# A two-layer hybrid decoder on one core: first phase, one gate block and the last products in another order, the last 256 rows written through transposes

## The chip, the cores and the metric

The kernel runs on one core of a Trainium2 chip. The metric is the device time of one execution in microseconds (us); lower is better. Engines are named as in the profile: PE is the matrix engine (TensorE), PEld its weight loads, DVE is VectorE, ACT is ScalarE, POOL is GpSimd and SP is SyncE, which here only issues DMAs. "L390" is line 390 of the kernel before.

## What is computed

The trunk has 1024 tokens, width 1024 and two layers; all in fp32. Cut to what matters here:

```
h = x
for layer in (0, 1):
    hn = rms_norm(h, mix_norm[layer])
    h  = h + (rg_lru_block(hn) if layer == 0 else stick_breaking_attention(hn))
    h  = h + swiglu_ffn(rms_norm(h, ffn_norm[layer]))
return rms_norm(h, final_norm)

rg_lru_block(x):                       # layer 0
    u = x @ w_in + b_in;  gate, rec = u[:1024], u[1024:]
    rec = causal depthwise conv of 4 taps over rec
    r, i = sigmoid(block-diagonal gates of rec, 4 blocks of 256)
    log_a = -8 * r * softplus(-lam);  a = exp(log_a);  b = sqrt(1 - a*a) * i * rec
    s[t] = a[t] * s[t-1] + b[t]
    return (gelu(gate) * s) @ w_out + b_out

swiglu_ffn(x): (silu(x @ w_gate) * (x @ w_up)) @ w_down          # 2816 wide
```

## The kernel before

**Data.** Activations are held transposed: a tile is 128 channels by 512 tokens. There are 8 channel tiles (d or k from 0 to 7) and two token halves n, so the residual stream is `h[d][n]`. Each fp32 operand is split into a high part (a copy on ACT, `whi`, `xh`, `rh`) and a low part (a subtraction on DVE, `wlo`, `xl`, `rl`), and each product is three matmuls (`mm3`, L124 to L127: high by high, high by low, low by high). An RMS norm is a sum of squares over channels: ACT squares, DVE adds the squares into an accumulator, PE sums over partitions (`column_stats`, L189), a chain of one ACT square root and six small DVE operations makes the factor per token (`rstd`, L158 to L167, into `rcol`), and PE spreads the factor over all partitions by multiplying it with the identity (`spread`, L172).

**First phase** (L245 to L320). All engines follow an order written out by hand. SP loads the eight x tiles of half 0 (`xr`) alternating with eight weight pieces (`fr`, the first four column tiles of `w_in`); ACT's queue loads the table of vectors `vc` (gains, biases). For each k, ACT and DVE split weights and x and PE multiplies half 0. Then PE does half 1 of the four tiles (`second(i, ks)`, 24 matmuls each), between which the two column sums and the two spreads are placed: sum 0, spread 0 after half a tile, sum 1 after one and a half tiles, spread 1 after two and a quarter. The norm is linear, so the tiles are multiplied by the factor (`rbc[n]`) afterwards.

**The RG-LRU stage** (L323 to L475). PE's order is a list of words written by hand (L472); the order of the other engines follows from a planner in the order of the program. A word is a letter and a number: `A` projects a recurrent tile (48 matmuls, unless the first phase did it), multiplies it by `rbc` (L400), runs the four taps (L402, L404) and splits the result (`rh` L406, `rl` L407). `G` is a gate block: it multiplies two recurrent tiles, 2b and 2b+1, with the gate weights (48 matmuls) and then needs a long chain of ACT and DVE operations for each, ending in a scan (L428 to L439). `B` projects a gate-branch tile, multiplies by `rbc` (L446) and applies gelu. `Y` multiplies scan and gelu (DVE). The order ends in

```
... A6 B3 Y3 G2 A7 B4 Y4 G3 B5 Y5 B6 Y6
```

after which `last_tile` (L454) projects B7 and rewrites `xh`, `xl` with the split products, tile by tile; the output projection (`ob_ps`) reads them. Weight tiles come from a ring of three pairs; PSUM has four tiles of 1024 columns, used in turn. The tiles of this stage, small ones included, lie in a pool `lp` over the memory of the first phase, and a tile waits until what lay there is no longer read. The small tiles hold the softplus constants (36 short DVE operations, L331 to L365).

**FFN and end.** The FFNs use a seven-product scheme of 2x2 blocks: a step of the second matrix (a "visit", `VISITS`) updates channel tiles d and d+4 in both halves with products 0 to 6. Products 0, 2, 4 and 5 use one PSUM bank in turn, so each waits until ACT or DVE has read the one before (`post_out`, L995). A channel tile that is complete is squared, added into `acc[n]` and multiplied by the final gain (`finished`, L984). In the last layer the last two visits, to tiles 3 and 7 and to tiles 0 and 4, are written out by hand: products 0, 1, 2, 4, 5 of visit 11 in a loop, the rest in `finish` (L1175 to L1230). There the last visit is done with plain products (`last`), first for half 0 (`first`), then for half 1 in two pieces of 256 tokens (`mid`, `end`); for each piece the factor is computed and spread, and `give` multiplies all eight channel tiles (DVE, or POOL for the tiles called slow) and stores them by SP. For `end` this is four matmuls (L1229), eight multiplications of 128x256 and eight stores, alternating between SP and ACT. The output is stored transposed as (8, 2, 128, 512).

Of the kernel before, what the change touches and what calls it, by code (L numbers as in the profile page):

```python
# [29 lines left out]
V_MIX, V_FFN, V_FIN, V_BIN, V_CW, V_CB, V_GB, V_LAM, V_BO = 0, 16, 32, 40, 56, 88, 96, 112, 120  # L30
FIRST = (ND, ND + 1, 0, ND + 2)
# [3 lines left out]
def trunk(  # L35
# [14 lines left out]
    nc = tc.nc  # L50
    f32 = lambda t: t.bitcast(F32)
# [192 lines left out]

    with ExitStack() as st, tc.manual_schedule(engines={E.PE, E.Activation, E.DVE, E.Pool, E.SP}):  # L245
# [7 lines left out]
        xr = [[one(f"xr{d}_{n}") for n in range(NH)] for d in range(ND)]  # L253
        nc.scalar.dma_start(vc, table)
        for k in range(ND):
            nc.sync.dma_start(xr[k][0], x[k, 0])
            nc.sync.dma_start(fr[k].rearrange("p (t c) -> p t c", t=4), lru_first[k])
# [17 lines left out]

        bank = half(pa[FIRST[3]], 1)
        for k in range(ND):
# [14 lines left out]
        for k in range(3):  # L292
            x_square(k, 1)

# [22 lines left out]
        second(2, range(2))  # L317
        spread_to(1)
        second(2, range(2, ND))
# [3 lines left out]
    with ExitStack() as st:  # L323
        lp = st.enter_context(tc.tile_pool(name="lp", bufs=1, reuse_waits="tile"))
        V = nc.vector
        lam = vc[:, V_LAM : V_LAM + ND]
        sm = lambda name: lp.tile([P, ND], F32, name=name)
# [12 lines left out]
        two = lp.tile([P, ND], I32, name="two")  # L340
# [15 lines left out]
        nbias = lp.tile([P, ND, 4], F32, name="nbias")  # L356
# [114 lines left out]
        with tc.manual_schedule(engines={E.PE}):  # L471
            for what in "A0 A1 B0 A2 B1 G0 A3 Y0 Y1 A4 B2 G1 A5 Y2 A6 B3 Y3 G2 A7 B4 Y4 G3 B5 Y5 B6 Y6".split():  # L472
                {"A": stage_a, "B": stage_b, "G": stage_g, "Y": stage_y}[what[0]](int(what[1]))
            mix = last_tile(ND - 1)
# [65 lines left out]
    def mix_out_ffn_in(h, mix, bias, layer, gnext, ob):  # L540
# [128 lines left out]
        with tc.manual_schedule(engines={E.PE, E.Activation, E.DVE, E.Pool}):  # L669
# [325 lines left out]
            def post_out(u, i, ps):  # L995
# [11 lines left out]
                if VISITS[u][2] == NF // 2 and i in ((1, 3, 6, 5) if final and u == NV - 2 else (1, 4, 6, 5)):  # L1007
# [3 lines left out]
            if final:  # L1011
                steps.pop()
# [3 lines left out]

            last_use = {p: max(u for u, (_, p0, p1) in enumerate(VISITS) if p0 <= p < p1) for p in range(NF // 2)}
            for s_, (kind, x) in enumerate(steps):
                w, nw, ahead = nw, nxt, None
                if s_ + 2 < len(steps):  # L1020
                    ahead = weights_of(*steps[s_ + 2])
                elif final and s_ + 2 == len(steps):
                    ahead = weights_out(NV - 1)
                    ahead.homes = held[1:]
                last_two = final and kind == "v" and x == NV - 2
# [15 lines left out]
                def tail(i, js):  # L1041
                    if i == 3:
                        banks[2] = pp.tile([P, NB], F32, tag="p", name=f"p{i}_ps")
                    part(banks[2], w, i, rhs[i], js, onto=i != 3)
                    if js[-1] == 2:
                        post_out(x, i, banks[2])
                        for dn in done:
                            finished(*dn)
                        del done[:]

                if last_two:
                    early = cp.tile([P, 4], F32, tag="rs_s", name="rs_s", bufs=2)
                    nc.scalar.sqrt(early[:, 0:1], ones)
                rest = [lambda: tail(3, range(3)), lambda js: tail(6, js)]
                for k, i in enumerate((0, 1, 2, 4, 5) if last_two else ORDER):
# [42 lines left out]
                    elif nw and last_two:  # L1098
                        if k == 3:
                            nw.a_lo()  # L1100
                            nw.r_hi()
                        elif k == 4:
                            nw.r_lo()
# [63 lines left out]
            if final:  # L1167
                finish(h, nw, R, pp, ob, held[0], *rest)
# [5 lines left out]

    def finish(h, w, R, pp, ob, rs, third, sixth):  # L1175
        d0, p0, p1 = 0, NF // 2 - 2, NF // 2


        def last(x, n, i0, i1, between=lambda: None, while_squared=lambda: None):
            d, cs = d0 + x * HK, slice(i0 * P, i1 * P)  # L1180
            ps = pp.tile([P, NB], F32, tag="p", name="o_ps")[:, cs]
            for k, p in enumerate(range(p0, p1)):
                for y in range(2):
                    hi, lo = w.a[("r", y) if x else y]
                    c = slice(k * P, (k + 1) * P)
                    rhs = [t[:, cs] for t in R[p][((0, 1), (7, 6))[n][y]]]
                    mm3(ps, hi[:, c], lo[:, c], *rhs, k + y == 0, k + y == 2)
            between()
            t, sq, ac = h[d][n][:, cs], rbc[n][:, cs], acc[n][:, cs]
# [392 lines left out]
```

## Time and profile before

| | us |
|---|---|
| median of three runs | 2222.49 (2217.23 to 2222.87) |
| profiled execution, device time | 2223.05 |
| its span, first to last instruction | 2221.3 |
| PE busy | 2172.0 (98%) |
| DVE busy | 1722.2 (78%) |
| ACT busy | 1147.8 (52%) |
| POOL busy | 224.2 (10%) |

The span is the distance from the first to the last instruction of one execution; 1.75 us of its device time lie outside. Times in the profile are counted from the start of the span. Busy time of PE counts each matmul to its modelled end, so that PE can be called busy while it runs at half clock.

### The profile page before, as it was taken

The numbers are of one execution on the slowest core, as the hardware profiler recorded it, in microseconds if no ns is written. First come the engines' busy times: TensorE is split into PE (matmuls) and PEld (weight loads), VectorE is DVE, ScalarE is ACT, GpSimd is POOL, SyncE is SP. The second block draws the span as 40 slices with busy tenths as digits, with TensorE's granted clock in tenths as the row PEclk, the third lists the DMA queues.
The fourth block names the chain that finished last, engine by engine and source line by source line (L and its number), as shares of the span: only waits on it lengthen the run. The fifth ranks groups of instructions, "written<-read, shape, count | busy, mean of one in ns | idle before, by whom it ended". The sixth has DMA issues, their size and how long they took to land.

```text
span 2221.3 us, 28188 instructions
## 1 busy us (share of the span) xinstructions
PE 2172.0 (98%) x10022; PEld 1798.9 (81%) x10022; DVE 1722.2 (78%) x2418; ACT 1147.8 (52%) x2030; POOL 224.2 (10%) x356
## 2 busy tenths in 40 slices
PE   8998999999999999999999999999999999999996
PEld 7787888888888888878888888778888888888885
DVE  6877678677777887868888888866876777788886
ACT  5567444444444554646666666653543444454464
POOL 0000020000000000003333333421000000000001
PEclk9999999999999999999999999999999999999998
DMA  4020312344444854443333333631133444466442
GB/s 172 21 63 31 133 40 70 108 126 146 142 156 133 284 185 120 151 133 86 89 93 99 101 87 104 196 118 57 48 113 118 149 142 147 152 234 226 135 136 81
DMA packets 132893, 273.51 MB, mean 123 GB/s; under 512 B 15376, under 2 KB 23696, under 8 KB 132752
## 3 DMA queue, kind: packets, MB, share of 16 engines
q1 hardware_dynamic: 132032, 271.12, 38.8%
q8 instruction: 79, 1.29, 0.2%
q10 hardware_dynamic: 720, 0.59, 0.1%
q14 instruction: 62, 0.51, 0.1%
HBM read 175.70 MB, written 70.78 MB: 111 GB/s over the span
## 4 chain that ended last, share of the span: by engine, by line
PE 80%; DVE 11%; ACT 5%; issue 2%; DMA 1%; SPq 0%; DVEq 0%; ACTq 0%
PE p_ps L127 18%; PE p_ps L125 18%; PE p_ps L126 17%; PE qk_ps L127 3%; PE qk_ps L125 3%; PE qk_ps L126 3%; PE ob_ps L125 2%; PE ob_ps L126 2%; PE ob_ps L127 2%; PE wt_ps L1404 2%; DVE F L1392 2%; PE a_ps L125 1%; PE a_ps L126 1%; PE a_ps L127 1%; PE z_ps L1367 1%
## 5 line engine op out<-in xcount | busy, mean ns | idle before, releaser
L1393 POOL TENSOR_TENSOR w<-w,F 128x128 f32<-128x128 f32 (+1 forms) x192 | 185.1, 965 | 316.7 <-DVE F L1390 179.5
L125 PE MATMUL p_ps<-vh,wbh 128*128 128x512 f32 x524 | 204.4, 390 | 1.4 <-ACT ta L1002 0.8
L125 PE MATMUL p_ps<-vh,wch 128*128 128x512 f32 x524 | 204.2, 390 | 0.8 <-ACT tb L1002 0.8
L127 PE MATMUL p_ps<-vh,wcl 128*128 128x512 f32 x524 | 204.1, 390 | 0.5 <-DVE wcl L629 0.5
L127 PE MATMUL p_ps<-vh,wbl 128*128 128x512 f32 x524 | 204.2, 390 | 0.0
L127 PE MATMUL p_ps<-vh,wal 128*128 128x512 f32 x524 | 204.1, 389 | 0.1
L126 PE MATMUL p_ps<-vl,wbh 128*128 128x512 f32 x524 | 203.9, 389 | 0.0
L126 PE MATMUL p_ps<-vl,wch 128*128 128x512 f32 x524 | 203.9, 389 | 0.0
L126 PE MATMUL p_ps<-vl,wah 128*128 128x512 f32 x524 | 203.9, 389 | 0.0
L125 PE MATMUL p_ps<-vh,wah 128*128 128x512 f32 x524 | 203.8, 389 | 0.0
L615 ACT CAST wbh<-sb 128x1024 fp32r<-128x1024 f32 (+2 forms) x69 | 69.6, 1009 | 192.6 <-DVE sb L599 192.6
L1413 ACT CAST th<-wt_ps 128x512 fp32r<-128x512 f32 x192 | 93.3, 486 | 72.2 <-PE wt_ps L1404 70.0
L1390 DVE TENSOR_TENSOR_SCAN F<-F,unit 128x128 f32<-128x128 f32 (+3 forms) x128 | 127.1, 994 | 4.5 <-ACT F L1386 4.5
L1414 DVE TENSOR_TENSOR tl<-wt_ps,th 128x512 fp32r<-128x512 f32 x192 | 105.1, 548 | 28.6 <-ACT th L1413 27.3
L125 PE MATMUL qk_ps<-vh,whi 128*128 128x512 f32 x264 | 118.9, 451 | 0.6 <-ACT vh L205 0.6
L125 PEld LDWEIGHTS p_ps<-vh,wbh 128*128 128x128 f32 x524 | 98.4, 188 | 22.4 <-ACT ta L1002 1.2
L127 PEld LDWEIGHTS p_ps<-vh,wcl 128*128 128x128 f32 x524 | 98.4, 188 | 21.8 <-DVE wcl L629 1.4
L127 PEld LDWEIGHTS p_ps<-vh,wbl 128*128 128x128 f32 x524 | 98.4, 188 | 21.8 <-DVE wbl L619 1.3
L125 PEld LDWEIGHTS p_ps<-vh,wch 128*128 128x128 f32 x524 | 98.4, 188 | 21.5 <-ACT tb L1002 1.3
L127 PEld LDWEIGHTS p_ps<-vh,wal 128*128 128x128 f32 x524 | 98.4, 188 | 21.4 <-DVE wal L610 1.0
L126 PEld LDWEIGHTS p_ps<-vl,wah 128*128 128x128 f32 x524 | 98.4, 188 | 20.4
L126 PEld LDWEIGHTS p_ps<-vl,wch 128*128 128x128 f32 x524 | 98.4, 188 | 20.4
(402 smaller groups left out, 5706.3 us busy)
## 6 DMA issues: line engine op xcount, KB each, us to landing
raw<-in_ffn_w_in SPq DMA_DIRECT2D x88, 512.0 KB, 3.8
vl<-pd SPq DMA_DIRECT2D x128, 256.0 KB, 3.7
pd<-U SPq DMA_DIRECT2D x90, 256.0 KB, 2.3
raw<-in_ffn_w_out SPq DMA_DIRECT2D x28, 512.0 KB, 4.0
raw<-in_attn_w_qkv SPq DMA_DIRECT2D x24, 512.0 KB, 3.6
acc<-pd SPq DMA_DIRECT2D x28, 256.0 KB, 2.7
pph<-rbc SPq DMA_DIRECT2D x28, 256.0 KB, 2.5
ppl<-acc SPq DMA_DIRECT2D x28, 256.0 KB, 2.6
```

The source lines that it names most:

```text
L125: nc.tensor.matmul(ps, lhsT=wh, rhs=mh, start=first, stop=False, **kw)
L126: nc.tensor.matmul(ps, lhsT=wh, rhs=ml, start=False, stop=False, **kw)
L127: nc.tensor.matmul(ps, lhsT=wl, rhs=mh, start=False, stop=last, **kw)
L615: nc.scalar.copy(self.full(self.wb), self.full(self.sb))
L1367: nc.tensor.matmul(ps[:, 0 : c1 - c0], lhsT=lhsT, rhs=KL[q][hx][:, c0:c1], start=False, stop=True)
L1390: nc.vector.tensor_tensor_scan(rev, rev, unit[:, NB - n :][:, ::-1], first, op0=ALU.mult, op1=ALU.add)
L1392: nc.vector.tensor_tensor_scan(rev, rev, rev, first, op0=ALU.mult, op1=ALU.bypass)
L1393: nc.gpsimd.tensor_mul(wt, wt, F[:, 1 : n + 1])
L1404: nc.tensor.transpose(tp[:, c : c + P], W[q, hx, j, kb // 4][:, (kb % 4) * P : (kb % 4 + 1) * P], ident)
L1413: nc.scalar.copy(th[:, q0:], tp[:, q0:])
L1414: nc.vector.tensor_sub(tl[:, q0:], tp[:, q0:], f32(th)[:, q0:])
```

## The change

1. **First phase.** The first weight piece `fr[0]` is issued on ACT's queue, ahead of the table, and no longer on SP's. PE gets eight products of the identity with itself ahead of the first real product. All squares and sums of half 1 come before the first `column_stats`. Sum 1 now comes after the first tile of half 1 and spread 1 half a tile later.
2. **Small tiles.** The small tiles of the RG-LRU stage get a pool of their own, `lc`, opened ahead of the first phase.
3. **Gate blocks.** `B5` moves ahead of `G3`, so that three tiles (A7, B4, B5) lie between G2 and G3.
4. **End.** Visits 11 and 12 are both in a new `finish`. Its products alternate: 0, 1, 2 of visit 11, tile 0 of visit 12 (half 0), 4, tile 4 (half 0), 5, 3, tile 0 (mid), 6, and so on. The squares go to a tile of their own. The last 256 tokens are not multiplied tile by tile: 16 transposes turn them into two row tiles of 128 tokens by 1024 channels in four PSUM banks, ACT and DVE multiply each bank by the token's factor on the way out (`rcol`, one number per partition), and four stores write rows.
5. **Output.** The output is one flat array: 768 tokens transposed, then 256 tokens as rows.

```diff
+        nc.scalar.dma_start(f4(fr[0]), lru_first[0])
         nc.scalar.dma_start(vc, table)
         for k in range(ND):
             nc.sync.dma_start(xr[k][0], x[k, 0])
-            nc.sync.dma_start(fr[k].rearrange("p (t c) -> p t c", t=4), lru_first[k])
+            if k:
+                nc.sync.dma_start(f4(fr[k]), lru_first[k])
...
         bank = half(pa[FIRST[3]], 1)
+        for i in range(8):
+            nc.tensor.matmul(bank[:, 0:P], lhsT=ident, rhs=ident, start=True, stop=True)
...
-        for k in range(3):
+        for k in range(ND):
             x_square(k, 1)
+            x_add(k, 1)
...
         column_stats(sacc[0], bank, 0)
-        for k in range(3, ND):
-            x_square(k, 1)
-        for k in range(ND - 2):
-            x_add(k, 1)
         second(0, range(4))
         spread_to(0)
-        for k in (ND - 2, ND - 1):
-            x_add(k, 1)
         second(0, range(4, ND))
+        column_stats(sacc[1], bank, 1)
         second(1, range(4))
-        column_stats(sacc[1], bank, 1)
+        spread_to(1)
         second(1, range(4, ND))
-        second(2, range(2))
-        spread_to(1)
-        second(2, range(2, ND))
+        second(2, range(ND))
         second(3, range(ND))
...
-        sm = lambda name: lp.tile([P, ND], F32, name=name)
+        sm = lambda name: lc.tile([P, ND], F32, name=name)
...
-... G2 A7 B4 Y4 G3 B5 Y5 B6 Y6
+... G2 A7 B4 Y4 B5 G3 Y5 B6 Y6
...
+                post = product(2)
+                post()
+                finished(d1, 0)
+                w.d_hi()
+                w.d_lo()
+                e.r_hi()
+                e.r_lo()
+                sq = rp.tile([P, D], F32, tag="raw", name="sq")
+                last(0, *first)
+                post = product(4)
+                summed(0, *first)
+                post()
+                last(1, *first)
+                post = product(5)
+                summed(1, *first)
+                post()
+                post = product(3)
+                finished(d1 + HK, 0)
+                post()
+                last(0, *mid)
+                stats(acc[0], pp, "p", 0)
+                finished(d1 + HK, 1)
+                summed(0, *mid)
+                post = product(6)
+                factor(*first)
+                give(*first, (), (3, 7))
+                post()
+                give(*first, (1, 2))
+                last(1, *mid)
+                finished(d1, 1)
+                give(*first, (5,))
+                summed(1, *mid)
+                last(0, *end)
+                give(*first, (0,), (4,))
+                summed(0, *end)
+                stats(acc[1], pp, "p", 1, 0, 2)
+                give(*first, (6,))
+                last(1, *end)
+                factor(*mid)
+                give(*mid, (), (3, 7))
+                summed(1, *end)
+                rows = [(hf, i, pp.tile([P, NB], F32, tag="p", name="e_ps")) for i in range(2, 4) for hf in range(2)]
...
+                turn((1, 2, 3))
+                give(*mid, (1, 2))
+                stats(acc[1], pp, "p", 1, 2, 4)
+                turn((0,))
+                ys = [rp.tile([P, D], F32, tag="raw", name="y") for _ in range(2)]
+                for k, (hf, i, ps) in enumerate(rows):
+                    y = half(ys[i - 2], hf)
+                    r = rcol[:, NT // 2 + i : NT // 2 + i + 1]
+                    if k % 2 == 0:
+                        nc.scalar.activation(y, ps, AF.Copy, scale=r)
+                    else:
+                        V.tensor_scalar_mul(y, ps, r)
+                    (nc.scalar if k % 2 else nc.sync).dma_start(
+                        out_r[(i - 2) * P : (i - 1) * P, hf * NB : (hf + 1) * NB], y
+                    )
+                    if k == 1:
+                        give(*mid, (5, 6), (0, 4))
```

In the new `finish`, `w` holds the weights of visit 11 and `e` those of visit 12; `last(x, n, i0, i1)` does tile 4x of visit 12, adds it into `h` and squares it, and `summed` adds the square and applies the gain. `turn(js)` transposes the 128x128 pieces of channel tiles j and j+4.

More of the change, by code (lines that the diff above doesn't have):

```diff
@@ L339, in trunk @@
             V.scalar_tensor_tensor(pq, pq, cf, gq, op0=ALU.add, op1=ALU.mult)
-        two = lp.tile([P, ND], I32, name="two")
+        two = lc.tile([P, ND], I32, name="two")
         V.tensor_scalar(two, kq, -8388608.0, 127.0 * 8388608.0, op0=ALU.mult, op1=ALU.add)
@@ L471, in trunk @@
         with tc.manual_schedule(engines={E.PE}):
-            for what in "A0 A1 B0 A2 B1 G0 A3 Y0 Y1 A4 B2 G1 A5 Y2 A6 B3 Y3 G2 A7 B4 Y4 G3 B5 Y5 B6 Y6".split():
+            for what in "A0 A1 B0 A2 B1 G0 A3 Y0 Y1 A4 B2 G1 A5 Y2 A6 B3 Y3 G2 A7 B4 Y4 B5 G3 Y5 B6 Y6".split():
                 {"A": stage_a, "B": stage_b, "G": stage_g, "Y": stage_y}[what[0]](int(what[1]))
@@ L1021, in mix_out_ffn_in @@
                     ahead = weights_of(*steps[s_ + 2])
[L1022 to L1025, printed above, removed]
+                    if final and s_ + 3 == len(steps):
+                        ahead.homes = held[1:]
                 g = {5: (0, 1), 6: (2, 3)} if s_ == 0 else {0: (1,), 1: (2,), 2: (3,)}
@@ L1040, in mix_out_ffn_in @@
                     rhs = {i: [R[p][i] for p in range(p0, p1)] for i in range(NPROD)}
[L1041 to L1055, printed above, removed]
+                for k, i in enumerate(ORDER):
                     b = BANK[i]
```

142 lines of the change are left out of this document (74 added, 68 removed).

## The prediction

> **What bounds the kernel now.** I read the page, then who waited for whom on PE, stage by stage, then the timeline around each wait. The page's line of busy times:
>
> ```profile
> PE 2172.0 (98%) x10022; PEld 1798.9 (81%) x10022; DVE 1722.2 (78%) x2418; ACT 1147.8 (52%) x2030; POOL 224.2 (10%) x356
> ```
>
> PE is the bound, and it is idle for only 2% of the span. The change takes no product out of the long middle, so what it can win is PE's waits in the stages that it touches, the slow clock behind them, and the stretch behind PE's last instruction. PE's waits from 0 to 100 us, from 100 to 250, and from 2150 to the end (total us, times, longest):
>
> ```profile
> PE a_ps L125 <- ACT xh L262: 5.9, 1, 5.9
> PE g_ps L125 <- ACT rh L406: 1.2, 1, 1.2
> PE g_ps L126 <- DVE rl L407: 0.8, 1, 0.8
> ...
> PE g_ps L125 <- ACT rh L406: 6.2, 1, 6.2
> PE g_ps L126 <- DVE rl L407: 0.5, 1, 0.5
> ...
> PE st_ps L191 <- DVE acc L1193: 3.5, 2, 1.9
> PE ob L172 <- DVE rcol L167: 2.2, 1, 2.2
> PE ob L172 <- DVE hh L1208: 2.1, 1, 2.1
> PE p_ps L125 <- ACT tb L1002: 1.5, 2, 0.8
> PE p_ps L125 <- ACT ta L1002: 1.4, 2, 0.8
> ```
>
> These are all of PE's waits there. G0 waits (1.2 + 0.8) and G3 (6.2 + 0.5). G1 and G2, each with three tiles between it and the gate block ahead, do not appear. The end waits 10.7. Two windows (length, then busy time of PE, PEld, DVE, ACT, POOL; granted clock; DMA) show G3's stretch and what lies behind PE's last row:
>
> ```profile
> 180.00:200.00 20.00, 13.37 (x52) 10.32 (x51) 19.70 (x17) 10.63 (x10) 0.00 (x0) 0.81 0.14 38
> ...
> 2214.30:2221.30 7.00, 0.00 (x1) 0.00 (x0) 2.08 (x6) 0.37 (x1) 1.41 (x2) 0.50 0.48 158
> ```
>
> At G3 the clock falls to 0.81 while DVE is full (19.70 of 20); at the end 7.0 pass without PE.
>
> **G3 and B5, the largest term.** PE's timeline (start, duration, instruction, idle before):
>
> ```profile
> 188.98 0.39 PE L127 MATMUL a_ps<-xh,wlo 128*128 128x512 f32 x1
> 189.20 0.39 PE L125 MATMUL g_ps<-rh,whi 128*128 128x512 f32 x1
> ...
> 196.21 0.79 PE L125 MATMUL g_ps<-rh,whi 128*128 128x512 f32 x1 [6.16 <-ACT rh L406]
> ...
> 198.06 0.63 PE L127 MATMUL g_ps<-rh,wlo 128*128 128x512 f32 x1
> ...
> 210.02 0.39 PE L125 MATMUL a_ps<-xh,whi 128*128 128x512 f32 x1
> ```
>
> At full speed products start about 0.227 apart (188.98 to 189.20, to a hundredth), so the block's 48 should take 10.9; it took 210.02 - 189.20 = 20.8. So 9.9 are lost: 6.6 of waits, and by subtraction 3.3 because the rows behind the wait run at half clock (0.63 long against 0.39). A7's parts, a weight split and the two ends of G3's chain:
>
> ```profile
> 195.11 1.04 ACT L406 CAST rh<-rec 128x1024 fp32r<-128x1024 f32 x1 [4.88 <-DVE rec L404]
> 196.19 1.22 DVE L407 TENSOR_TENSOR rl<-rec,rh 128x1024 fp32r<-128x1024 f32 x1
> ...
> 190.04 1.20 DVE L116 TENSOR_TENSOR wlo<-raw,whi 128x1024 fp32r<-128x1024 f32 x1
> ...
> 205.95 1.23 DVE L431 TENSOR_TENSOR gs<-gs,rec 128x1024 f32<-128x1024 f32 x1 [6.08 <-ACT gs L429]
> 226.97 2.29 DVE L439 TENSOR_TENSOR_SCAN y<-ga,gs 128x1024 f32<-128x1024 f32 x1
> ```
>
> With B5 in between, PE works from 189.2 to 200.1. A7's parts are complete at 196.15 and 197.41, so G3 no longer waits. B5's weights were split at 190.04; now they come ahead of G3's in the ring and get the slot of G2's weights, free since PE left G2, while G3's gate weights get the later place, done by 191.2 and wanted at 200.1. The whole 9.9 goes.
>
> Late next: the output projection. In the old times G3 ends at 211.0, 1.0 later than before, but only B6 and the last tile (2 x 10.9) follow, so the projection begins at 232.8 instead of 210.0 + 3 x 10.9 = 242.7. It wants the last split part of half 0 seven k steps (0.68 each) later, at 237.6. Rows for what lies on the way:
>
> ```profile
> 201.32 1.28 ACT L428 ACT_TABLE_LOAD   x1 [2.71 <-PE g_ps L127]
> 202.62 1.11 ACT L428 ACTIVATE ga<-g_ps,vc 128x1024 f32<-128x1024 f32 x1
> ...
> 227.36 1.16 ACT L447 ACTIVATE gb<-gb,vc 128x1024 f32<-128x1024 f32 x1
> ...
> 231.98 1.29 DVE L446 TENSOR_TENSOR gb<-a_ps,rbc 128x512 f32<-128x512 f32 x2 [1.60 <-PE a_ps L127]
> 236.19 1.89 DVE L466 TENSOR_TENSOR xl<-y,xh 128x512 fp32r<-128x512 f32 x3
> ```
>
> From 200.1 on ACT waits for B5's eviction (1.3), loads a table, does the gelu, loads again and does three activations of 1.1: G3's chain starts at 208.4 instead of 205.95. It took until 229.26, 23.3; B5's eviction and one weight split (2.5) no longer lie inside it, so it ends at about 229.2 again. By 237.6 DVE then still owes B6's eviction and Y6 (2.5), B7's eviction and product of half 0 (1.3), a weight split (1.2) and eight parts (0.6 each): 9.8, to 239.0, or 1.4 late. I take 1.5 back; bounds 0 (DVE slips small pieces into pauses of the chain) and 4 (the second weight tile also falls behind). **Term: -9.9 + 1.5 = -8.4** (-5.9 to -9.9).
>
> The Trainium skill, "ScalarE: Activation LUTs", section What ACT_TABLE_LOAD costs, counts a load of 1.28 and a drain of about 1.38, 2.66 for each switch. By that two switches would start the chain 2.8 later and the term would be about -5.6. The trace does not show the drain: the activation above starts 1.30 after its load.
>
> **G0 and the first phase.** G0's waits are 1.9. Why A1 is late:
>
> ```profile
> 46.77 0.69 DVE L302 COPY rbc<-a_ps 128x512 f32<-128x512 f32 x1 [3.73 <-PE a_ps L172]
> 51.34 0.17 DVE L331 SCALAR_TENSOR_TENSOR az<-vc 128x8 f32<-128x8 f32 x1 [3.88 <-PE a_ps L126]
> ```
>
> Spread 1 stands 18 products further forward, so its copy comes 4.1 earlier, at 42.7. Then DVE waited 3.88 for PE, because the small tiles lie over weight pieces that PE still reads; with `lc` that goes. A0 and A1 start about 8 earlier, where 2 are wanted. What the move costs: seven sums of half 1 (0.6 each, 4.2) stand ahead of sum 0's chain on DVE, and PE waits for that chain at spread 0, half a tile (2.7) later. The weight splits that DVE can put off (wanted from G0 and B1 on) cover it; without that cover it is 1.5. **Term: -1.9** (-0.4 to -2).
>
> The start:
>
> ```profile
> 1.18 0.42 SPq L257 DMA_DIRECT2D fr<-in_lru_first  x1
> ...
> 4.59 0.62 ACT L278 CAST fh<-fr 128x512 fp32r<-128x512 f32 x1 [2.13 <-DMA fr<-in_lru_first]
> ...
> 5.88 0.80 PE L125 MATMUL a_ps<-xh,fh 128*128 128x512 f32 x1 [5.88 <-ACT xh L262]
> ...
> 11.52 0.43 PE L125 MATMUL a_ps<-xh,fh 128*128 128x512 f32 x1
> ```
>
> The piece was issued second on SP; now it goes first on ACT's queue, one issue (0.42) sooner, but the table, which x's high part needs, goes one later. Gain 0 to 0.4; I take 0.4. The eight identity products last 2.4 at half clock (the row of 2213.08 below has four in 1.22), then PE idles about 2 until the data come. Full speed came 5.6 after the first product here and 6.6 after 196.21, so 2.4 of work and a pause should hardly hasten it. Bounds: nothing, or full clock from the first product on, half of 5.6. I take 0.3, near the first. **Term: -0.7** (0 to -3.2).
>
> **The end.** PE's first row behind the shared products, its last two groups, the last factor and the last multiplications; below, transposes in the attention stage:
>
> ```profile
> 2176.30 0.50 PE L125 MATMUL p_ps<-vh,wbh 128*128 128x512 f32 x1 [0.75 <-ACT ta L1002]
> ...
> 2209.93 1.01 PE L191 MATMUL st_ps<-ones,acc 128*128 128x1 f32 x4 [1.55 <-DVE acc L1193]
> 2213.08 1.22 PE L172 MATMUL ob<-ident,rcol 128*128 128x128 f32 x4 [2.14 <-DVE hh L1208]
> ...
> 2212.20 0.16 DVE L167 TENSOR_TENSOR rcol<-rs_s,rs_t 128x2 f32<-128x2 f32 x1
> 2214.74 2.08 DVE L1208 TENSOR_TENSOR hh<-hh,ob 128x256 f32<-128x256 f32 x6 [1.72 <-ACT held L1199]
> ...
> 1201.28 0.60 PE L1404 MATMUL wt_ps<-ident,w 128*128 128x128 f32 x4
> ```
>
> From 2176.30 to 2214.30 PE spends 38.0, of which 10.7 - 0.8 = 9.9 waiting and 28.1 working. Removed: the last spread, 1.2. Added: 16 transposes, at 0.11 each about 1.8 (four end within 0.60). The alternation puts other products between those that share a bank and between a tile and its sum, so PE restarts less often: I take 1 for that. Work 27.7. Stepping through the new order with durations like those above leaves waits of about 3.5: 0.8 where the first tile of visit 12 waits for its low weights behind four DVE operations, 2 at the sum of `mid`, 0.7 at its spread. Product 2 starts 0.9 later, because the square and gain left from the visit before now go ahead of the table load on ACT. PE ends at 2177.2 + 27.7 + 3.5 = 2208.4; the last sum starts 1.1 earlier, at 2207.3, and from sum to factor it is 2212.36 - 2209.93 = 2.4, so 2209.7. Two evictions on DVE (0.69, as in the row of L302) with two multiplications of 0.4 between take 2.1, ACT's two (half of 1.11 each) less: 2211.8. Before, from the last multiplication (2216.8) to the end of the span it was 4.5, with eight stores behind the factor; now four follow, but SP's stand behind stores of tiles that POOL multiplies. I take 4: 2215.8. **Term: -5.5** (-3 if the waits stay at 6; -8.5 if there are none).
>
> **Sum.** -8.4 - 1.9 - 0.7 - 5.5 = -16.5. The profiled execution took 2223.05, 0.6 above the median, so 2206.5 by it and **2206** against the median of 2222.49.
>
> **Rivals.** (a) DVE becomes the bound: G3's wait returns as one of about 5.5 at the output projection. For: no slack is left in the arithmetic above. Against: bits of DVE work can fill pauses. 2206 + 4 = 2210. (b) The identity products bring the clock up early and DVE keeps up: 2.5 and 1.5 more, and 2 at the end: 2200. (c) The clock falls at the end: PE pauses there and 16 transposes at half clock take 1.8 more: 2208. The four rows of 2213.08 took 1.22 against 0.60 for four transposes among other products; no row shows transposes alone. The Trainium skill, "TensorE: Matmul & The Clock Gate", Part 4, says that a transpose does not count as activity for the clock, which speaks for (c). (d) Slower: at the output projection DVE comes later than PE at each of its first four products, by 2 each, and each pause brings half clock as behind 196.21, 3.3 more: 4 x 5.3 = 21, so 2227. It decides from four pauses on; against it, DVE makes a part in 0.6 and PE uses one in 0.68, so DVE should catch up. (e) The move does nothing, because A7's parts slip as far as G3 does: 2206 + 8.4 = 2214.
>
> **Chances.** Forecast 0.56, (a) 0.18, (b) 0.12, (c) 0.06, (d) 0.04, (e) 0.04. Below 0.3% (6.7 us, about what a measurement here can tell from no change) counts as the same, so faster ends at 2215.8. The forecast, (a), (b), (c) and (e) lie there; 0.05 is left for the edges of (a) and (e) beyond it. Faster 0.91, same 0.05, slower 0.04. All terms at their ends give -9.3 and -23.6, 2213 and 2199; I go one lower for (b), whose clock gain could fall together with an end without waits: 2198 to 2213. That leaves out (d), (e) and some edges.
>
> **What would show it.** Right: no PE wait over 1 at G3, and matmul rows of 0.39 from G0 to the output projection; the operations on `lc` tiles before 46 us; PE waits below 5 in the last 40 us; no spread for the last 256 tokens; a first real product near 5.5 and rows of 0.63 for 5 us behind it. Wrong: a wait at `ob_ps` over 3 (a), several of them (d), rows of 0.39 before 9 us (b), transposes 0.2 apart (c), G3 still waiting for `rh` (e), a wait at spread 0 (the G0 term).

## The result: no difference that can be measured

The changed kernel took 2217.72 us (median of 19 runs, 2214.07 to 2220.24), the kernel before on the same chip 2218.75 (19 runs, 2214.69 to 2222.87): ratio 0.9993, 95% interval 0.9985 to 1.0. Forecast were 2206 and a range from 2198 to 2213. G0's and G3's waits are gone as forecast, and nearly all of the gain is lost again, most of it at a place that no part of the prediction names. The profiled execution took 2218.56 (span 2216.8). The page's line of busy times:

```profile
PE 2177.2 (98%) x10050; PEld 1805.3 (81%) x10050; DVE 1721.9 (78%) x2412; ACT 1152.7 (52%) x2033; POOL 224.1 (10%) x356
```

PE is no less busy than before (2172.0). Its waits in the same three stretches as before (total us, times, longest):

```profile
PE a_ps L129 <- DVE xl L272: 1.6, 1, 1.6
PE a_ps L285 <- POOL ident masks.py:199: 1.4, 1, 1.4
PE a_ps L175 <- DVE rcol L170: 1.2, 1, 1.2
PE a_ps L128 <- ACT xh L269: 1.1, 1, 1.1
...
PE a_ps L130 <- DVE wlo L119: 5.6, 1, 5.6
PE ob_ps L129 <- DVE xl L467: 0.2, 1, 0.2
...
PE st_ps L194 <- DVE acc L1047: 3.1, 1, 3.1
PE p_ps L128 <- ACT ta L1003: 2.0, 1, 2.0
```

No row for `rh` or `rl` is left: the moves did what they say. New are a wait of 1.6 at the second real product, one of 1.2 at spread 0, and one of 5.6 for the low part of a weight tile. PE's timeline at the start, around that last wait, and at the end:

```profile
1.36 3.78 PE L285 MATMUL a_ps<-ident 128*128 128x128 f32 x16 [1.36 <-POOL ident masks.py:199]
6.20 0.80 PE L128 MATMUL a_ps<-xh,fh 128*128 128x512 f32 x1 [1.06 <-ACT xh L269]
8.57 0.80 PE L129 MATMUL a_ps<-xl,fh 128*128 128x512 f32 x1 [1.58 <-DVE xl L272]
...
103.90 0.39 PE L129 MATMUL a_ps<-xl,whi 128*128 128x512 f32 x1
109.84 0.79 PE L130 MATMUL a_ps<-xh,wlo 128*128 128x512 f32 x1 [5.56 <-DVE wlo L119]
110.44 0.63 PE L128 MATMUL a_ps<-xh,whi 128*128 128x512 f32 x1
...
2201.26 1.01 PE L194 MATMUL st_ps<-ones,acc 128*128 128x1 f32 x4 [3.15 <-DVE acc L1047]
...
2205.69 2.60 PE L1124 MATMUL e_ps<-ident,hh 128*128 128x128 f32 x12
```

The stop at 109.84 is B2's third product, the first that needs the low part. From 109.84 to 115.56 stand 13 products; at 0.227 apart they would take 2.95, they take 5.72. With the wait the place costs 5.6 + 2.8 = 8.3.

The account up to the output projection: the first gate product comes 4.0 later (71.03 against 67.00: a later start, the wait of 1.6 for x's low part, and the wait at spread 0), G0's waits are 1.9 less, B2 is 8.3 more, G3 is 9.9 less: +0.5. Measured is +0.1: the first product of `ob_ps` starts at 242.78, before at 242.66. All that the change won by then is gone.

**Why B2's weights are late.** ACT's splits of weights in the kernel before, then in the changed one (A4's, then B2's), then DVE's low parts in the changed one:

```profile
66.98 1.05 ACT L112 CAST whi<-raw 128x1024 fp32r<-128x1024 f32 x1 [4.80 <-PE a_ps L126]
85.73 1.03 ACT L112 CAST whi<-raw 128x1024 fp32r<-128x1024 f32 x1
```

```profile
72.62 1.16 ACT L448 ACTIVATE gb<-gb,vc 128x1024 f32<-128x1024 f32 x1 [5.34 <-DVE u L399]
...
86.61 1.04 ACT L115 CAST whi<-raw 128x1024 fp32r<-128x1024 f32 x1
...
93.35 1.04 ACT L115 CAST whi<-raw 128x1024 fp32r<-128x1024 f32 x1
```

```profile
87.98 1.22 DVE L119 TENSOR_TENSOR wlo<-raw,whi 128x1024 fp32r<-128x1024 f32 x1
...
106.78 1.28 DVE L405 SCALAR_TENSOR_TENSOR rec<-u,vc,rec 128x1024 f32<-128x1024 f32 x1
...
108.57 1.22 DVE L119 TENSOR_TENSOR wlo<-raw,whi 128x1024 fp32r<-128x1024 f32 x1
```

Before, ACT splits A4's weights at 66.98, as soon as B1 has left their slot, and B2's at 85.73. Now A4's split stands behind G0's chain, at 86.61, although B1 has left the slot by 71.0 and ACT is idle until 72.62. B2's split comes at 93.35, 7.6 later than before. Its low part comes 21 later (87.22 before): it waits on DVE behind the work on A3 and A4 until 108.57, although its high part is ready at 94.4. So what costs is the low part's place on DVE. ACT and DVE take their order from the planner here. That the planner puts the low part there because A4's split moved is argued, not shown: no run moves one without the other.

Which part of the change moved the split, the traces tell. It stands ahead of G0's chain with the swap alone (65.70), with the new end alone (66.51) and, on a kernel with swap and end, with the order of the first phase (70.16), the DMA order (67.20) or the identity products (66.02). The new pool `lc` of the small tiles alone puts it behind (85.60); taken out of the changed kernel, it lets the split go back (70.28).

### The profile page after: what moved, and what is told of

Read it like the earlier page. It is cut to its first block, busy times and chain, and to the rows that moved or that the text cites. A ratio compares the mean times of both kernels' runs of the same rounds, so it can differ in the third digit from the quotient of the medians.

```text
span 2216.8 us, 28236 instructions
## 1 busy us (share of the span) xinstructions
PE 2177.2 (98%) x10050; PEld 1805.3 (81%) x10050; DVE 1721.9 (78%) x2412; ACT 1152.7 (52%) x2033; POOL 224.1 (10%) x356
## 4 chain that ended last, share of the span: by engine, by line
PE 83%; DVE 9%; ACT 4%; DMA 2%; issue 1%; SPq 1%; DVEq 0%; ACTq 0%
PE p_ps L130 18%; PE p_ps L128 18%; PE p_ps L129 18%; PE qk_ps L130 3%; PE qk_ps L128 2%; PE qk_ps L129 2%; PE ob_ps L129 2%; PE ob_ps L128 2%; PE ob_ps L130 2%; PE wt_ps L1454 2%; PE a_ps L130 2%; PE a_ps L128 2%; PE a_ps L129 2%; DVE F L1442 2%; PE z_ps L1417 1%
## 5 line engine op out<-in xcount | busy, mean ns | idle before, releaser
L128 PEld LDWEIGHTS p_ps<-vh,wah 128*128 128x128 f32 x524 | 98.4, 188 | 20.3
```

The costliest lines, as they stand in the source:

```text
L128: nc.tensor.matmul(ps, lhsT=wh, rhs=mh, start=first, stop=False, **kw)
```

## Experiments

All times are medians; the kernel before had 2216.9 to 2220.3 in the sets of runs below. A ratio is to the kernel before in the same set. Medians of different sets are compared below too; there a difference of 2 or less is not sure, since the kernel before differs by up to 3.4 between the sets.

### 1. The changed kernel with the small tiles back in `lp`

```diff
-        sm = lambda name: lc.tile([P, ND], F32, name=name)
+        sm = lambda name: lp.tile([P, ND], F32, name=name)
```

(and the same for `two` and `nbias`)

> The changed kernel, with the small tiles of the constant chain back in the pool `lp` (the one part of the change that makes the planner put the split of A4's weights, on ScalarE, behind G0's chain instead of ahead of its second half). Theory T (the planner's later split of A4's weights is what makes the new wait of 5.6 us at 109.8 and the 6.8 us of half clock behind it): the wait at 109.8 is gone and the clock stays full from 13 to 950, so 5.6 + 3.4 = 9 come back; G0's wait for `rh` and `rl` returns with at most 1.9. Time 2209 to 2211 where the changed kernel has 2218. Rival U (the sums of half 1 and the earlier chain of the first phase load VectorE so that any order has a late low part): the wait at 109.8 stays within 1 us, time 2217 to 2219. Rival V (the wait only moves to a later gate block): the wait near 110 goes but one of 4 to 6 stands between 120 and 250, time 2215 to 2219.

2208.95 (ratio 0.995, 0.9938 to 0.9962). Theory T holds: no wait at B2, and 8.8 less than the changed kernel. G0's waits are back, and the wait at spread 0 is now 3.4:

```profile
PE a_ps L175 <- DVE rcol L170: 3.4, 1, 3.4
...
PE g_ps L128 <- ACT rh L408: 1.2, 1, 1.2
...
PE g_ps L129 <- DVE rl L409: 0.8, 1, 0.8
```

### 2. Each part alone on the kernel before

Only `lc`:

> The kernel before, with nothing changed but the pool of the small tiles of the constant chain (`lc` beside the first phase instead of `lp` over it). Theory T: G0's waits (1.9) go, and a wait of 4 to 6 us for a low weight part appears near 105 to 115 with 6.8 us of half clock behind it; G3's wait stays. Time about 2218.75 - 1.9 + 9 = 2226. Rival U: no wait near 110, G0's gone, time 2216.5 to 2217.

2227.04 (1.0035, 1.0026 to 1.0045). PE's waits for low parts, at the start and from 100 to 250:

```profile
PE a_ps L126 <- DVE xl L266: 2.6, 1, 2.6
...
PE a_ps L127 <- DVE wlo L116: 5.6, 1, 5.6
```

So the part that was to win 1.9 costs 7 to 8 by itself. The second wait is the one at B2. The first was not expected: it is the subject of experiment 6. G3's wait for `rh` is 3.6 in this run, where it was 6.2, so part of the loss is hidden there.

Only B5 ahead of G3:

> The kernel before, with nothing changed but B5 ahead of G3. Prediction's term: -8.4 (-5.9 to -9.9), since no wait for `rh` stands at G3 and the clock stays full: 2209 to 2213, forecast 2210.3. From the trace of the changed kernel, where the projection waited only 0.2: the whole -9.9, 2208.9. Rival (the term was never there, since the planner gives the time back at the projection): a wait of 3 or more at the projection and 2214 or more.

2210.02 (0.9955, 0.9942 to 0.9968): 9.5 less. The projection's waits are 0.9 and 0.2, against the 5.5 of rival (a).

Only the new end:

> The kernel before, with nothing changed but the end (products of visits 11 and 12 alternating, last 256 rows by transposes, the output's layout). Prediction's term: -5.5 (-3 to -8.5), 2213.3. From the two traces, where the stretch behind product 1 of visit 11 shrank from 45.7 to 43.2: -2.6, 2216. Rival (the end gains nothing that holds over runs, the 2.6 is the clock's window): within 1 of 2218.75. In each case a wait for `acc` near 3 at the second sum and one near 2 at product 2 are expected, as in the trace of the changed kernel.

2215.86 (0.9982, 0.9974 to 0.9991): 3.6 less, with the two expected waits of 3.1 and 2.0.

### 3. Swap and end together, then the start part by part

> The kernel before with B5 ahead of G3 and the new end; the first phase, its DMAs and the small tiles as before, no identity products. If the terms add up as measured one by one (swap -9.5, end -3.6): 2206.4 where before has 2219.5, and so 2.5 less than the changed kernel with its small tiles in `lp` (2208.95), whose first phase then costs 2.5. Rival (the first phase of the change is worth its forecast once the late split is gone): 2209 or more, and the terms do not add.

2207.17 (0.9946, 0.9933 to 0.9959). The two terms add to within 1. On this kernel the parts of the first phase were put one at a time.

Its order (eight squares and seven sums ahead of sum 0's chain):

> As the kernel with swap and end, with only the order of the first phase as in the change (eight squares and seven sums of half 1 ahead of sum 0's chain, spread 1 half a tile behind spread 0); DMAs and small tiles as before, no identity products. Prediction: the splits of the weights give way on VectorE and the sums cost nothing, 2207.2 as without. From the trace of the changed kernel with its small tiles in `lp`, where three low parts of weights (1.2 each) stood between the sums and spread 0 waited 3.4 for `rcol`, with 3.4 us of half clock behind the wait: +3 to +5, 2210 to 2212.

2212.82, or 5.6 more, where the prediction had nothing. DVE's timeline ahead of sum 0's chain, then PE's at spread 0:

```profile
26.65 1.22 DVE L119 TENSOR_TENSOR wlo<-raw,whi 128x1024 fp32r<-128x1024 f32 x1
27.79 0.68 DVE L277 TENSOR_TENSOR sacc<-sacc,sq 128x512 f32<-128x512 f32 x1
28.39 1.22 DVE L119 TENSOR_TENSOR wlo<-rawg,whi 128x1024 fp32r<-128x1024 f32 x1
29.53 0.68 DVE L277 TENSOR_TENSOR sacc<-sacc,sq 128x512 f32<-128x512 f32 x1
30.13 1.22 DVE L119 TENSOR_TENSOR wlo<-raw,whi 128x1024 fp32r<-128x1024 f32 x1
31.26 3.07 DVE L277 TENSOR_TENSOR sacc<-sacc,sq 128x512 f32<-128x512 f32 x4
34.25 0.15 DVE L196 TENSOR_SCALAR ms<-a_ps 128x4 f32<-128x4 f32 x1
```

```profile
35.80 1.13 PE L175 MATMUL a_ps<-ident,rcol 128*128 128x128 f32 x8 [2.41 <-DVE rcol L170]
```

The three low parts of weights do not give way: they stand between the sums. The chain starts at 34.25, in the kernel with swap and end alone at 30.74, and spread 0 waits 2.4. Behind it and behind G0's unchanged waits the clock is down (granted clock 0.50 from 37.0 to 40.3 and from 74.6 to 77.8), where the kernel without the new order kept full clock at both: each time some 1.7.

The first piece on ACT's queue:

> As the kernel with swap and end, with the first weight piece first on ScalarE's queue and the table behind it, no identity products. Prediction's term: -0.4 to 0. From the trace of the changed kernel, where the table landed at 5.34 instead of 4.02 and the first product waited 1.6 more: +0.3 to +2 us, 2207 to 2208.5, and the table as the last of the first pieces to land.

2208.59, 1.4 more, but the five runs (2206.89 to 2211.83) reach below those without (2207.07 to 2207.65), so only the row is sure: the first product starts at 6.09 instead of 5.69. The table lands at about 5.3 instead of 3.9, and now x's high part waits for it. The prediction saw this mechanism and had the sign of the sum wrong.

The eight identity products:

> As the kernel with swap and end, with the eight identity products ahead of the first phase, and nothing else of the new first phase. Prediction's term (0.3, bounds 0 to 2.8): 2206.1. Theory W (the clock is set for stretches of 3.41 us by whether PE was busy through the stretch before; the identity products fill 1.4 to 5.1, a whole stretch only in the runs in which one happens to begin before about 1.7): some runs 2 to 2.5 shorter, median 0 to 2.5 below the kernel without them, 2204 to 2206.4. Rival (identity products count for nothing): the same median within 0.7, and first products at 0.63 in the profile.

2204.85, 2.3 less. Not for the reason given: in the profile the first real product is as early (5.67 against 5.69) and takes 0.79 in both. Some 0.9 of it is a wait of the projection's first tile for `gb` (at 238.84), which is gone: here the same product starts at 237.72, while DVE is not done with `gb` before 238.7. Why it need not wait, the traces do not say. Another 1.7 is a stretch of half clock at 962, which the one profile has and the other has not.

### 4. Nine identity products

> As the kernel with swap, end and identity products (2204.85), with nine of them instead of eight, so that PE is busy from 1.4 on without the pause of 0.5 ahead of the first product. Theory W (the clock goes up behind the first stretch of 3.41 us in which PE was busy throughout): full clock at 4.8 to 8.2 in every run, where the kernel with eight had 9.67 in its profile, 0.7 to 2.4 us less of the time: 2202.5 to 2204.1. Rival (products on the identity do not count, as a transpose does not by the Trainium skill, "TensorE: Matmul & The Clock Gate", Part 4): full clock at 9 to 13, the time as with eight or 0.1 longer.

2203.16 (0.9938, 0.9925 to 0.995). PE's first rows:

```profile
1.36 3.82 PE L281 MATMUL a_ps<-ident 128*128 128x128 f32 x18 [1.36 <-POOL ident masks.py:199]
5.67 0.50 PE L128 MATMUL a_ps<-xh,fh 128*128 128x512 f32 x1 [0.49 <-ACT xh L265]
6.45 0.50 PE L129 MATMUL a_ps<-xl,fh 128*128 128x512 f32 x1 [0.28 <-DVE xl L268]
6.79 0.39 PE L130 MATMUL a_ps<-xh,fl 128*128 128x512 f32 x1
```

The clock is full from 4.6, ahead of the first real product, as theory W has it, so identity products do raise it. In the profiles of all seven kernels with nine of them full clock came at 4.5 to 7.6; with eight it came anywhere from 4.2 (experiment 7) and 5.2 (experiment 1) to 9.7 (the kernel above), 13.2 (the changed kernel) and 13.9 (experiment 5). In the late ones PE pauses ahead of the first product, and in the last two it waits for x's low part as well; that these pauses are the reason is argued. In every trace the clock changes at distances that are multiples of 3.41 (in the changed kernel at 13.21, 108.78 and 115.61, 28 and 2 times 3.413 apart); where the changes lie differs from run to run. The Trainium skill, "TensorE: Matmul & The Clock Gate", Part 1, says just this: a free-running window of 3413 ns, and full clock after a busy one. The traces agree on the length. They do not fit the same page's advice in "Why this matters for your kernels" to leave no pauses above about 3 us, if shorter ones are taken for safe: 2.4 at spread 0 in experiment 3, and 1.2 + 0.8 at G0 there, were enough for half clock. How much of the 1.7 between the medians is the ninth product stays open, since the runs overlap (2202.85 to 2205.39 with nine, 2202.82 to 2205.41 with eight).

### 5. B2's low part on GpSimd, in the changed kernel

```diff
-            w = load_cols(lru_w_in[j])
+            w = load_cols(lru_w_in[j], nc.gpsimd if j == 2 else None)
```

(the second argument is the engine of the low part)

> The changed kernel with one instruction on another engine: the low part of B2's weights is computed by GpSimd, which is idle here, instead of VectorE, where it ended at 108.6 and was wanted at 104.3. Theory T (the new wait is that one low part queued behind VectorE's other work): wait and half clock behind 109.8 gone, 2209 (2218 - 9), as with the small tiles in `lp`, and G0's waits gone too. Rival V (the stage as a whole is short of VectorE; the next low part is then late): a new wait of 3 to 6 between 110 and 235, 2213 to 2218.

2208.25 (0.9955, 0.9942 to 0.9967), 9.5 less than the changed kernel. GpSimd did the 128x1024 subtraction in 2.71, at 94.29, long before it was wanted. One instruction on an idle engine removes the whole loss, and no other wait of PE takes its place: rival V falls. It is not free for DVE, though. The scan that runs beside it takes 4.51, where it took 2.28 in the changed kernel:

```profile
94.65 4.51 DVE L440 TENSOR_TENSOR_SCAN y<-ga,gs 128x1024 f32<-128x1024 f32 x1
```

So DVE is spared 1.22 and loses 2.2, which nothing waits for here.

### 6. Two prices of `lc`

`lc` and B2's low part on GpSimd, on the kernel with swap, end and eight identity products:

> As the kernel with swap, end and identity products (2204.85), with the small tiles in `lc` and the low part of B2's weights on GpSimd. Theory T (the `lc` part takes G0's 2.0 away, and its price is the one late low part): no wait at G0, none over 1 up to the projection, 2202.9. Rival V (with the old first phase the stage is short of VectorE at another place): a new wait of 2 or more between 66 and 235, 2205 or more.

2207.91, 3.1 more than without. G0's waits are gone and none stands at B2, but PE waits 2.7 for the first low part of x. DVE's first rows:

```profile
3.84 0.17 DVE L335 SCALAR_TENSOR_TENSOR az<-vc 128x8 f32<-128x8 f32 x1 [3.84 <-DMA vc<-in_table]
...
5.36 1.37 DVE L343 SCALAR_TENSOR_TENSOR pq<-pq,gq 128x8 f32<-128x8 f32 x7
...
7.49 0.69 DVE L287 TENSOR_TENSOR fl<-fr,fh 128x512 fp32r<-128x512 f32 x1
...
8.18 0.74 DVE L269 SCALAR_TENSOR_TENSOR xl<-xr,vc,xh 128x512 fp32r<-128x512 f32 x1
```

With memory of its own the chain of small operations may start as soon as the table has landed, and the planner does start it there: at 3.84, ahead of the first low parts, which are wanted at 5.0. In the changed kernel the same (5.36) makes the wait of 1.6 at its second product. Then the chain was written out by hand behind sum 1:

```diff
         column_stats(sacc[1], bank, 1)
+        az, kq, gq, pq, cc, ch = ...; first 16 operations of the chain
         second(1, range(4, ND))
         second(2, range(2))
         spread_to(1)
+        the other operations of the chain
```

> As the kernel with swap, end and nine identity products (2203.16), with the small tiles in `lc` and the constant chain written out by hand on VectorE, its first 16 operations between sum 1's chain and spread 1's copy, the rest behind that copy: it can neither slip ahead of the first low parts (as it did wherever the planner placed it on `lc`: 2.7 us of wait at the first products) nor stand between A0's evictions. B2's low part stays on VectorE; the planner's order still has A4's split behind G0's chain. Theory T (late split and early chain are two separate prices of `lc`): no wait at the start, none at G0 (-2.0), but the wait of 4 to 6 at B2 near 105 with 6.8 us of half clock: 2203.2 - 2.0 + 9 = 2210. Rival (the late split hurts only together with the early chain): no wait near 105, 2201.

2211.27 (0.9968, 0.9956 to 0.998). No wait at the start, none at G0, 5.5 at B2: two separate prices, as theory T says. The split is late here too, with the chain out of its way, so the chain's place is not the reason; A0's and A1's earlier work may be, which no run shows.

### 7. What the end still loses

The square root later, and the last products ahead of the second sum:

> As the kernel with swap, end and identity products (2204.85), with two rows of the end moved: the early square root, and with it the load of its table, behind the splits for product 2 instead of ahead of product 1's eviction; and the last product group (rows 768 to 1023 of the second tile) ahead of the second sum instead of behind it. Theory (these are the two waits by which the end missed its forecast, 2.0 at product 2 and 3.1 at the sum): the wait at product 2 falls to about 0.6, the last products fill the wait for `acc` at full clock, and the end is 1.4 + 2 shorter: 2201.5. Rival (the stores set the end, since the last SP stores leave 1.9 behind the last multiplication): PE ends earlier, the span by less than 1.5: 2203.5 or more.

2205.11, where 2204.85 was the kernel without. Product 2's wait fell to 0.5, 1.5 less. The other move gave it back: PE's last products end 6.2 earlier, and then PE waits for DVE at two places instead of one:

```profile
PE ob L175 <- DVE hh L1066: 3.1, 1, 3.1
PE st_ps L194 <- DVE acc L1051: 1.7, 1, 1.7
```

Twelve identity products in front of the second sum:

> As the kernel with swap, end and nine identity products (2203.16), with the early square root behind the splits for product 2 (-1.4, as its wait fell from 2.0 to 0.5), and twelve products on the identity, whose result nobody reads, in front of the second sum, where PE waits 3.1 for `acc`. Theory C (the end missed its forecast because the clock falls behind that wait): the clock stays full to the last stretch, the last twelve products take 1.4 instead of 2.7 and the sixteen transposes 1.8 instead of 3.4, and the end is 1.4 + 2.9 shorter: 2198.9. Rival (VectorE's operations and the stores behind them set the end, not PE's rows): PE's rows shorten as in C, the time by 1.4 to 2.4 alone: 2200.8 to 2201.8.

2200.98 (0.9926, 0.9913 to 0.9938): what the rival expects. The rows do what theory C says, sum, last products and transposes:

```profile
2181.41 2.84 PE L1119 MATMUL d_ps<-ident 128*128 128x128 f32 x24
2184.72 0.61 PE L194 MATMUL st_ps<-ones,acc 128*128 128x1 f32 x4 [0.46 <-DVE acc L1051]
...
2188.42 1.47 PE L1131 MATMUL e_ps<-ident,hh 128*128 128x128 f32 x12
```

Twelve transposes take 1.47 at full clock, 2.60 in the changed kernel. But of the 2.2 less, 1.5 are the square root by its row (the wait at product 2 falls from 2.0 to 0.5), so the fill is worth about 0.7. Part of what PE's rows win is lost behind them, in the last factor's chain:

```profile
2189.07 2.78 POOL L1064 TENSOR_TENSOR hh<-hh,held 128x256 f32<-128x256 f32 x4 [5.89 <-ACT held L1057]
...
2191.22 0.65 DVE L168 TENSOR_TENSOR rs_t<-rs_t,ms 128x2 f32<-128x2 f32 x1
```

Two small operations of that chain, 0.16 each in the changed kernel, take 0.28 and 0.65 here, now that the chain runs beside GpSimd's last multiplications. All later kernels have the same 0.6. Behind PE's last row 8.5 pass to the end of the span, in the changed kernel 7.7.

Why the second sum waits 3.1 and not 2: DVE's row in the changed kernel, with GpSimd beside it.

```profile
2195.95 3.78 POOL L1060 TENSOR_TENSOR hh<-hh,held 128x512 f32<-128x512 f32 x3 [637.00 <-ACT held L1053]
...
2198.53 1.75 DVE L205 TENSOR_TENSOR acc<-acc,rbc 128x512 f32<-128x512 f32 x1 [1.00 <-ACT rbc L204]
```

The sum takes 1.75 and ends 0.55 behind GpSimd's third multiplication; the same sum takes 0.68 at 2193.53. With that multiplication (tile 4) on DVE:

> As the kernel with all that gained and without the fill (2200.37), with one multiplication of the end on VectorE instead of GpSimd (tile 4 of the first half). In the trace of the changed kernel the sum `acc` ahead of the second sum took 1.75 instead of 0.68 while GpSimd did that multiplication. Theory P (VectorE's operation on two SBUF tiles stood still until GpSimd's was done): the `acc` operation takes 0.68 again, the wait at the second sum falls from 3.1 to 2.0, and PE's rows end 1.1 sooner; the time 0.5 to 1.1 less, 2199.3 to 2199.9. Rival (the long operation waits for its own data): it stays at 1.7 and the wait at 3.1; the time 0 to 0.6 more for the multiplication moved to VectorE.

2200.73 where 2200.37 was without. The row is as theory P says, the time is not:

```profile
2182.44 0.69 DVE L205 TENSOR_TENSOR acc<-acc,rbc 128x512 f32<-128x512 f32 x1 [1.00 <-ACT rbc L204]
```

```profile
PE st_ps L194 <- DVE acc L1051: 2.1, 1, 2.1
PE ob L175 <- DVE hh L1066: 1.6, 1, 1.6
```

The sum's wait is 1.0 shorter and the wait at the next spread 1.2 longer (0.4 in the kernel without), since DVE now has the multiplication to do. The Trainium skill, "SBUF — State Buffer", section SBUF: two separate sides, says that DVE and GpSimd lock a pair of ports against each other for a whole instruction when DVE reads two SBUF tiles; the 1.75 against 0.69 agrees. So do the scan of experiment 5 (4.51 against 2.28) and the small operations above.

With eight identity products in the wait that is left:

> The same with eight identity products in front of the second sum (the wait that is left, 2.0, at 0.24 each). Theory C and P together: 2199.47 - 0.5 to 1 = 2198.5 to 2199. Rival (the end is set by VectorE and the stores): 2199.5 within 0.5.

2200.02, which is 0.55 above 2199.47: at the edge of the rival's band, and not the 0.5 to 1 less of theories C and P. Shorter rows of PE gain little at the end; VectorE's operations, held up in part by GpSimd, and the stores behind them set the time. These runs do not separate the two.

### 8. What gained, together

> What the runs point to, together: swap, end, nine identity products, the small tiles in `lc` with the chain by hand, B2's low part on GpSimd, and the early square root behind the splits for product 2. Terms: 2203.16 - 2.0 (G0's waits) - 1.4 (product 2) = 2199.8, no PE wait over 1 between the first product and the end's sum. Rival V (the stage is short of VectorE): a new wait of 2 or more between 66 and 235, 2202 or more.

2200.37 (0.9921, 0.9909 to 0.9933), 0.6 above the sum of its terms. From the first real product to the end of the RG-LRU stage the list of PE's waits has one row left:

```profile
PE ob_ps L129 <- DVE xl L471: 0.2, 1, 0.2
```

With the fill of twelve:

> All that gained, together: the kernel of the last row (2200.37) with the twelve identity products in front of the second sum. By the two kernels measured apart the fill is worth what the square root leaves of 2203.16 - 2200.98, 0.7: 2199.7. Rival (the end is set by VectorE and the stores, and the fill only shortens rows that wait later): the same within 0.5.

2199.47 (0.9921, 0.9907 to 0.9934), the fastest kernel here: 0.8% below the kernel before and 18 below the changed one. The fill alone is worth 0.9 here; at a ratio that is the same in both sets this is not told from nothing.

## Why the prediction was wrong

**G3 and B5: right.** -8.4 was forecast, -9.5 was measured alone. The projection was to take back 1.5; PE's waits there are 1.1 in experiment 2 and 0.2 in the changed kernel. DVE caught up, as the argument against rival (a) said.

**G0 and the first phase: the step that failed**, twice. First: "The weight splits that DVE can put off (wanted from G0 and B1 on) cover it; without that cover it is 1.5." The cover was never there: the three low parts stand between the sums (experiment 3), the wait is 2.4, and half clock behind the waits makes 5.6 of it, more than three times the price named for the missing cover. Second: the small tiles' move was priced as a gain alone, 1.9 of waits less. G0's waits did go. But freeing a memory wait changes what the planner sees, and so every order behind it: the chain went ahead of the first low parts (2.6 to 2.7 by itself, 1.6 in the changed kernel), and B2's low part went behind DVE's work on A3 and A4, with A4's split behind G0's chain (8.3). The prediction priced the operations that moved and not the ones that the planner would move for them. Its list of signs shows the gap: "the operations on `lc` tiles before 46 us" came true, at 5.4 us, which was part of the damage.

**The start: wrong in sign.** 0.4 was taken for the weight piece's earlier issue; it was seen that the table goes one place later, but not priced. x's high part needs it, and the first product comes 0.3 to 0.4 later. The identity products' clock, 0.3 forecast with 2.8 as a bound, came true only in some runs. Their length was misread: a product of the identity leaves two records, so the four records in 1.22 were two products. The eight took 3.78 instead of 2.4, and the pause behind them was 1.1 instead of about 2.

**The end: mechanism right, term too large.** -5.5 forecast; from product 1's last row to the end of the span it was 45.75 and is 43.15, so -2.6; -3.6 alone. The waits were sized right: product 2 waits 2.0 instead of 1.65, and the waits behind it are 3.15, of 3.5 forecast. The work was not: 27.7 was taken and PE needs 30.3. What failed here is the full clock that was taken for the work behind the waits. The 3.15 come in one piece, and behind that piece the clock is half (0.50 from 2201.3 to 2208.0): the last twelve products take 2.7 where the same work took 1.4, the sixteen transposes 3.2 where 1.8 was taken. That is rival (c), which had a chance of 0.06. Its cause is the wait and not the transposes, which run at 0.12 apart, all sixteen at full clock, as soon as the wait is filled. But shorter rows of PE gain less than 1 beyond the square root; that the end hangs on VectorE and what follows it, the stepping through missed.

**The chances.** Rival (a) named the right engine, VectorE, and the wrong place; no rival had a wait between G0 and G3, because the stage between them had no wait before. The parts measured one by one (-9.5, -3.6, +5.6, +1.4, -2.3, and +8.8 for `lc`) add to +0.4; the changed kernel is at -1.0.

## What to carry to other kernels

Where a planner orders part of the work, an edit that takes a wait away changes the order of all that it plans; price it by asking what can now start early and what is then pushed back, and compare the new orders of the engines, not only the instructions that moved. A cover counts only if the covering work is shown to move out of the way. Behind a pause of PE look for half clock: here it added half of the pause or more where it came (2.8 to 5.6 at B2, 3.3 to 6.6 at G3 before). Work moved to an idle engine can slow its neighbour: look at what runs beside it.

## What was not expected of the hardware

- The clock changes on a grid of 3.41 us that differs from run to run, and pauses well below that length bring it down in some runs: 1.2 + 0.8 at G0 cost nothing in the kernel before and a stretch of half clock (0.50 from 74.6 to 77.8) in the kernel of experiment 3 with the new order.
- Beside a GpSimd instruction a VectorE sum of two tiles took 1.75 instead of 0.68, a scan 4.51 instead of 2.28, and an operation on 128x2 elements 0.65 instead of 0.16.
- GpSimd does a 128x1024 subtraction in 2.71 where VectorE takes 1.22.
